# The inversion of 32-blocks in a gated DeltaNet layer: wider scratch transfers, and right operands stored transposed

## The chip, the cores and the metric

The kernel runs on one core of a Trainium2 chip. The metric is the device time of one execution in microseconds; what counts is the median of several runs. All data are fp32; the matrix engine's operands are fp32 too, the large products being split into a high and a low part.

## The reference, cut to what matters

One encoder layer works on a prompt of 1024 tokens and a sample of 256 tokens. A combined projection feeds a bidirectional gated DeltaNet (4 heads, 128 wide) and a differential attention; an output projection, two layer norms and a SwiGLU follow. The change concerns the DeltaNet. Its delta rule is, per head and direction:

```python
decay = jnp.exp(jnp.where(incl, gc[..., :, None] - gc[..., None, :], -jnp.inf))
kb = k * beta[..., None]
m = jnp.where(strict, jnp.einsum('bhnid,bhnjd->bhnij', kb, k) * decay, 0.0)
a_mat = m + jnp.eye(CHUNK, dtype=jnp.float32)
...
sol = lax.linalg.triangular_solve(a_mat, rhs, left_side=True, lower=True, unit_diagonal=True)
...
attn = jnp.einsum('bhnid,bhnjd->bhnij', q, k) * decay
```

A scan over the chunks then carries a 128 x 128 state. So every chunk needs the inverse of a unit triangular matrix.

## The kernel before

**Stages.** Phase A (`phase_a`) projects the input and prepares the DeltaNet: q, k, v, decays, and for every chunk the inverse; the chunk of the kernel has 128 tokens. Phase B runs the scans (`chain`, L974) and the differential attention side by side, phase C the output projection, then the feed-forward part. Phases share on-chip memory: tiles of phase B lie where tiles of phase A lay, and wait for their last reader.

**One preparation.** There are five preparations, one after the other: the four heads of the prompt (8 chunks each) and, as the fifth, the sample, whose 4 heads of 2 chunks are packed as 8 chunks. The texts call them the first to the fifth head. Each has 8 chunks and 2 directions, hence 16 matrices N of 128 x 128, and goes through three generators.

1. The front (`prep_front`, `prep_group`): convolved q, k, v are transposed on TensorE and normalised. Then, for each of two groups of 4 chunks, TensorE forms k·k and k·q in PSUM (L418, tile kq_ps), ScalarE copies them out scaled by -beta (L424) and once unscaled (L426), into the four slots of the tile KQ. The decays are made in place: the cumulated gates are broadcast by DMA into e_f and e_n (L395), masked on VectorE (L406) and exponentiated on ScalarE (L403); e_b is a second masked copy of e_n. VectorE multiplies decays and KQ into N (L435) and into the two attention matrices (L441), which go to the scratch `rec`. The four diagonal 32 x 32 blocks of N go to the scratch `nblk`, one DMA per direction, group and block (L438): 16 a head. kd, the scaled keys, also goes to `rec` (L454).
2. The block inversion (`invert_blocks`): all 64 blocks of 32 x 32 are loaded into the tile Wb with one block per partition, twice (L465), so that 128 partitions work. VectorE builds the inverse U by doubling: 2, 4, 8, 16. Each step is two products by `prod` (L468 to L471): an elementwise multiplication into itmp (L470) and a sum over the last axis (L471); the first product goes into the small tile T, the second into U. The right operand of the first product is a part of U (for 16, copied to R at L495), that of the second is T. Both are held in rows and read by columns: the last axis of the operand has a step of 8 elements (in R and T) or 32 (in U).
3. The levels (`spread_blocks`, `invert_levels`): U goes to the scratch `ublk` (L508), and so does its transpose, which is made in Wb (L509, L510). Both are loaded into the diagonal of the tiles UD, one DMA per orientation, block and direction (L514): 16 a head. Small TensorE products (L535) join 32-blocks to 64 and 64-blocks to 128, with copies between (L545, L559, L565, L572, L573), VectorE scales one result by -beta (L575), and four stores (L578) bring the inverses to `rec`.

**Order.** `advance` moves each of the three lines one step, after each projection block and in its middle; a new block inversion begins when the line is free, and a front goes on to its groups only when fewer than two inversions are under way (`room`). Within this, the order of the instructions on each engine, and of the DMAs on the issue queue of SyncE (SP), is laid out by a planner that follows a simulated timeline (`schedule_with_timeline_sim`), ready instructions with the earliest place in the program first; on the chip each engine and queue keeps that order. The scratch DMAs named above all go through SP. Wb, T, R, U, itmp, UD, KQ and the e tiles have one buffer, N two per direction.

**The end of phase A.** The scans of phase B read `rec` (L969); the first of these loads go into memory that the inversion's tile Z held before.

Of the kernel before, what the change touches and what calls it, by code (L numbers as in the profile page):

```python
# [16 lines left out]
P = 128  # L17
# [317 lines left out]
def prep_front(k, si, vh, c3, G, N, flag, room):  # L335


    nc, V, A, PO = k.nc, k.nc.vector, k.nc.scalar, k.nc.gpsimd
    gp = k.gp1
    raw = gp.tile([P, 2, 8, P], F32, tag="raw", name="raw")  # L340
    ss = gp.tile([P, 2, 8], F32, tag="ss", name="ss")
    for g in range(2):
        u0 = 4 * g
        for role in (0, 1, 2):
            ps = k.pt.tile([P, 512], F32, tag="tp", name="nat_ps")
            for i in range(4):
# [8 lines left out]
        sq = gp.tile([P, 16, P], F32, tag="kq", name="sq")[:, 0:8]  # L355
# [12 lines left out]
    yield  # L368
    while not room():
        yield  # L370
    N.extend(k.gp2.tile([P, 8, P], F32, tag=f"N{d}", name=f"N{d}") for d in range(2))
    for g in range(2):
        yield from prep_group(k, si, vh, g, raw, G, N)


def prep_group(k, si, vh, g, raw, G, N):
    nc, V, A, PO = k.nc, k.nc.vector, k.nc.scalar, k.nc.gpsimd
    rec = k.S.rec[si][vh][g]
    u0 = 4 * g
# [30 lines left out]
    masked(e_f, e_f, k.upper, ALU.add)  # L410
    decay(e_f, 0, 1.0)
    yield
    KQ = gp.tile([P, 4, 4, P], F32, tag="kq", name="KQ")
    for j in range(2):
        ps = k.pg.tile([P, 512], F32, tag="gp", name="kq_ps")
        for i in range(2):
            u = 2 * j + i
            nc.tensor.matmul(ps[:, i * 256:(i + 1) * 256], lhsT=kqT[:, u, 0, :],  # L418
                             rhs=kqT[:, u, :, :].rearrange("p a b -> p (a b)"), start=True, stop=True)
        for i in range(2):  # L420
            u = 2 * j + i
# [12 lines left out]
    def to_blocks(d, e):
        V.tensor_tensor(out=N[d][:, u0:u0 + 4, :], in0=KQ[:, :, 2 * d, :], in1=e, op=ALU.mult)  # L435
        for b in range(4):
            r = slice(32 * b, 32 * b + 32)
            nc.sync.dma_start(out=k.S.nblk[si][vh][d, u0:u0 + 4, b].rearrange("u r c -> r u c"), in_=N[d][r, u0:u0 + 4, r])  # L438

    def attn(d, e):  # L440
        V.tensor_tensor(out=e, in0=KQ[:, :, 1 + 2 * d, :], in1=e, op=ALU.mult)  # L441
        nc.sync.dma_start(out=rec[:, :, 1 + 6 * d, :], in_=e)
# [15 lines left out]
def invert_blocks(k, si, vh):  # L458
# [29 lines left out]
    yield  # L488
    for m in range(2):
        b = m * 528  # L490
        prod(8, 8, 8, (Wb, b + 8, [[32, 8], [0, 8], [1, 8]]), (U, b + 264, [[0, 8], [1, 8], [32, 8]]), (T, 0, [[8, 8], [1, 8]]))
        prod(8, 8, 8, (U, b, [[32, 8], [0, 8], [1, 8]]), (T, 0, [[0, 8], [1, 8], [8, 8]]), (U, b + 8, [[32, 8], [1, 8]]))
    yield
    for hf in range(2):
        V.tensor_copy(view(R, 0, [[8, 16], [1, 8]], 64 * hf, 64), view(U, 528 + 8 * hf, [[32, 16], [1, 8]], 64 * hf, 64))  # L495
    for a in (0, 8):
        prod(8, 8, 16, (Wb, 16 + a * 32, [[32, 8], [0, 8], [1, 16]]), (R, 0, [[0, 8], [1, 8], [8, 16]]), (T, a * 8, [[8, 8], [1, 8]]))
    yield
    for a in (0, 8):
        prod(8, 8, 16, (U, a * 32, [[32, 8], [0, 8], [1, 16]]), (T, 0, [[0, 8], [1, 8], [8, 16]]), (U, 16 + a * 32, [[32, 8], [1, 8]]))  # L500
    return Wb


def spread_blocks(k, si, vh, Wb):

    nc, V, U = k.nc, k.nc.vector, k.Ub
    V.tensor_copy(view(U, 24, [[32, 16], [1, 8]], 0, 64), view(U, 16, [[32, 16], [1, 8]], 64, 64))
    nc.sync.dma_start(out=k.S.ublk[si][vh][0].rearrange("d u b r c -> (d u b) (r c)"), in_=U[0:64])  # L508
    V.tensor_copy(Wb[0:64].rearrange("p (a b) -> p a b", a=32), U[0:64].rearrange("p (b a) -> p a b", a=32))  # L509
    nc.sync.dma_start(out=k.S.ublk[si][vh][1].rearrange("d u b r c -> (d u b) (r c)"), in_=Wb[0:64])  # L510
    for t in (1, 0):
        for b in range(4):
            for d in range(2):
                nc.sync.dma_start(out=diag(k, d, t, b), in_=k.S.ublk[si][vh][t][d, :, b].rearrange("u r c -> r u c"))  # L514


def diag(k, d, t, b):

    c = 32 * b if d == t else 32 * (b % 2)
    return k.UD[d][t][32 * b:32 * b + 32, :, c:c + 32]  # L520


def invert_levels(k, si, vh, N, G):

    nc, V, A, PO = k.nc, k.nc.vector, k.nc.scalar, k.nc.gpsimd
    q = [slice(32 * b, 32 * b + 32) for b in range(4)]
    hq = [slice(32 * (b % 2), 32 * (b % 2) + 32) for b in range(4)]
    uq, dq = (q, hq), (hq, q)
    lo, up = slice(0, 64), slice(64, 128)
    ub = (up, lo)  # L530

    def pe(ps, rows, c0, m, fn):
        for u in range(8):
# [34 lines left out]
    U, D = k.UD[0]  # L568
    r0 = pe(ps, lo, 0, 64, lambda u: (Z[up, 0, u, :], U[up, u, ub[0]]))
    Ub, Db = k.UD[1]  # L570
    r1 = pe(ps, up, 0, 64, lambda u: (Ub[up, u, ub[1]], Z[up, 1, u, :]))
    A.copy(U[lo, :, up], r0)  # L572
    A.copy(Db[up, :, lo], r1)  # L573
    off = 4 * NT[si] + (vh * 8 if si == 1 else 0)
# [17 lines left out]
def phase_a(k):  # L592
    nc, tc = k.nc, k.tc
    with ExitStack() as es:
# [65 lines left out]
        def prep(si, vh, c3):  # L660
# [999 lines left out]
```

## Time and profile before

| | us |
|---|---|
| median of 3 runs | 1794.15 |
| lowest and highest | 1793.14, 1796.1 |
| the profiled execution | 1791.56 |
| its span in the profile | 1789.8 |
| TensorE busy in the span | 1710.3 |
| VectorE busy | 1214.0 |
| ScalarE busy | 783.7 |

In the profile, PE is TensorE's matmul, PEld its weight load, DVE is VectorE, ACT ScalarE, POOL GpSimd and SPq the DMA issue queue of SyncE. A row names line, engine, operation, the written tile, an arrow and the tiles read. Rows of groups end with the count, the busy time in us and the mean of one in ns, and behind a second bar the engine's idle time ahead of them. Rows of a timeline begin with start and duration in us; a bracket gives idle time ahead of the instruction and what ended it.

### The profile page before, as it was taken

The numbers are of one execution on the slowest core, as the hardware profiler recorded it, in microseconds if no ns is written. First come the engines' busy times: TensorE is split into PE (matmuls) and PEld (weight loads), VectorE is DVE, ScalarE is ACT, GpSimd is POOL, SyncE is SP. The second block draws the span as 40 slices with busy tenths as digits, with TensorE's granted clock in tenths as the row PEclk, the third lists the DMA queues.
The fourth block names the chain that finished last, engine by engine and source line by source line (L and its number), as shares of the span: only waits on it lengthen the run. The fifth ranks groups of instructions, "written<-read, shape, count | busy, mean of one in ns | idle before, by whom it ended". The sixth has DMA issues, their size and how long they took to land.

```text
span 1789.8 us, 27447 instructions
## 1 busy us (share of the span) xinstructions
PE 1710.3 (96%) x10234; PEld 1483.0 (83%) x10234; DVE 1214.0 (68%) x2092; ACT 783.7 (44%) x1538; POOL 218.5 (12%) x201
## 2 busy tenths in 40 slices
PE   8999989999986899999999999999999999999998
PEld 8988868888864898788888888888888887888886
DVE  4245888986694468977665866665666665666696
ACT  4146766664433767877113332322222223553330
POOL 2000000000022435732321000000000000000011
PEclk9999999998985999999999999999999999999999
DMA  7124456656754977634631534333344432975541
GB/s 237 40 57 115 126 131 168 168 168 182 190 154 103 297 238 220 177 118 156 188 119 51 193 112 140 120 121 133 124 145 146 146 113 100 386 272 177 174 159 71
DMA packets 254116, 279.05 MB, mean 156 GB/s; under 512 B 49297, under 2 KB 198687, under 8 KB 252575
## 3 DMA queue, kind: packets, MB, share of 16 engines
q1 hardware_dynamic: 244079, 265.20, 47.6%
q10 hardware_dynamic: 9904, 12.10, 2.0%
q8 instruction: 80, 1.31, 0.3%
q14 instruction: 53, 0.43, 0.1%
HBM read 183.80 MB, written 93.43 MB: 155 GB/s over the span
## 4 chain that ended last, share of the span: by engine, by line
PE 54%; ACT 1%; DVE 1%; issue 1%; DMA 0%; POOLq 0%; POOL 0%; DVEq 0%; SPq 0%; ACTq 0%
PE dn_ps L1503 14%; PE gy_ps L1277 9%; PE gs_ps L1277 7%; PE om_ps L172 6%; PE gx_ps L1277 6%; PE gz_ps L1277 6%; PE gp_ps L1277 2%; PE o_ps L875 1%; PE x_ps L1182 0%; ACT ap L839 0%; PE s_ps L835 0%; PE tt_ps L862 0%; PE s_ps L836 0%; DVE ast L837 0%; ACT woh L1162 0%
## 5 line engine op out<-in xcount | busy, mean ns | idle before, releaser
L1293 ACT CAST sph<-wraw 128x512 fp32r<-128x512 f32 x92 | 57.0, 623 | 195.7 <-PE gy_ps L1277 124.5
L310 POOL TENSOR_TENSOR rs_r<-lva,mhalf 128x1 f32<-128x1 f32 x20 | 29.5, 1475 | 837.4 <-DVE lva L1139 818.9
L172 PE MATMUL dps<-xh,wlo 128*128 128x512 f32 (+1 forms) x552 | 122.7, 363 | 2.0 <-DVE wlo L163 2.0
L172 PE MATMUL dps<-xl,whi 128*128 128x512 f32 (+1 forms) x552 | 122.4, 364 | 0.0
L172 PE MATMUL dps<-xh,whi 128*128 128x512 f32 (+1 forms) x552 | 122.2, 362 | 0.0
L1293 ACT CAST sph<-wsum 128x512 fp32r<-128x512 f32 x80 | 49.7, 622 | 156.6 <-PE gy_ps L1277 61.9
L1503 PE MATMUL dn_ps<-tth,ssh 128*128 128x512 f32 x280 | 108.9, 389 | 0.0
L1503 PE MATMUL dn_ps<-ttl,ssh 128*128 128x512 f32 x280 | 108.8, 389 | 0.0
L172 PEld LDWEIGHTS dps<-xh,wlo 128*128 128x128 f32 x552 | 94.4, 193 | 17.3 <-DVE wlo L163 2.4
L1503 PE MATMUL dn_ps<-tth,ssl 128*128 128x512 f32 x280 | 108.1, 389 | 0.0
L172 PEld LDWEIGHTS dps<-xl,whi 128*128 128x128 f32 x552 | 94.8, 195 | 15.8 <-ACT whi L162 0.4
L172 PEld LDWEIGHTS dps<-xh,whi 128*128 128x128 f32 x552 | 94.1, 193 | 14.4
L329 DVE SCALAR_TENSOR_TENSOR c<-pad,cw,c 128x1024 f32<-128x1024 f32 (+1 forms) x96 | 81.7, 876 | 28.8 <-ACT c L327 28.3
L837 DVE TENSOR_REDUCE ast<-s_ps 128x1 f32<-128x1024 f32 (+1 forms) x80 | 83.5, 1055 | 22.6 <-PE s_ps L836 20.4
L1294 DVE TENSOR_TENSOR spl<-wraw,sph 128x512 fp32r<-128x512 f32 x92 | 63.0, 686 | 47.9 <-PE gs_ps L1277 29.6
L839 ACT ACTIVATE ap<-s_ps,ast 128x1024 f32<-128x1024 f32 (+1 forms) x80 | 79.8, 1000 | 34.7 <-DVE ast L837 32.1
L1294 DVE TENSOR_TENSOR spl<-wsum,sph 128x512 fp32r<-128x512 f32 x80 | 55.0, 688 | 46.8 <-issue 20.4
L835 PE MATMUL s_ps<-akl,aq 128*128 128x512 f32 (+1 forms) x144 | 65.8, 458 | 20.3 <-ACT ap L839 19.0
L1494 ACT CAST ssh<-sraw 128x640 fp32r<-128x640 f32 x77 | 55.9, 727 | 48.5 <-PE dn_ps L1503 34.3
L1495 DVE TENSOR_TENSOR ssl<-sraw,ssh 128x640 fp32r<-128x640 f32 x77 | 62.9, 820 | 16.8 <-ACT ssh L1494 13.4
L851 POOL TENSOR_TENSOR ap<-ap,ap 128x512 f32<-128x512 f32 (+2 forms) x60 | 62.4, 1059 | 81.2 <-ACT ap L848 49.5
L875 PE MATMUL o_ps<-av,tt 128*128 128x128 f32 x544 | 66.2, 280 | 0.0
(391 smaller groups left out, 4307.6 us busy)
## 6 DMA issues: line engine op xcount, KB each, us to landing
ld<-rec SPq DMA_DIRECT2D x160, 192.0 KB, 3.9
sraw<-hs SPq DMA_DIRECT2D x77, 320.0 KB, 4.7
wraw<-in_w_gate_up_dram SPq DMA_DIRECT2D x22, 1024.0 KB, 5.2
wraw<-in_w_in_dram SPq DMA_DIRECT2D x24, 512.0 KB, 4.2
wdraw<-in_w_down_dram SPq DMA_DIRECT2D x11, 1024.0 KB, 4.9
ws<-wdraw SPq DMA_DIRECT2D x11, 1024.0 KB, 3.9
traw<-ws SPq DMA_DIRECT2D x44, 256.0 KB, 4.1
araw<-dqk SPq DMA_DIRECT2D x40, 256.0 KB, 5.0
```

The costliest lines, as they stand in the source:

```text
L172: nc.tensor.matmul(out, lhsT=a(i), rhs=b(i), start=start and j == 0, stop=stop and j == len(seq) - 1)
L329: V.scalar_tensor_tensor(out=out, in0=pad[:, so + w:so + w + n], scalar=k.cw[:, w * 12 + ti:w * 12 + ti + 1], in1=out, op0=ALU.mult, op1=A ...
L835: nc.tensor.matmul(ps[:, o:o + w], lhsT=a.q[m][:, qs], rhs=a.kl[m][:, k0 + o:k0 + o + w], start=True, stop=False)
L837: V.tensor_reduce(out=st[:, m:m + 1], in_=ps, op=ALU.max, axis=AX.X, negate=True)
L839: A.activation(p, ps, AF.Exp, bias=st[:, m:m + 1], accum_out=a.s0[:, i:i + 1] if m == 0 else st[:, 2:3])
L851: nc.gpsimd.tensor_tensor(out=pr[0][:, c], in0=pr[0][:, c], in1=pr[1][:, c], op=ALU.add)
L875: nc.tensor.matmul(ps[:, j * P:(j + 1) * P], lhsT=tt[:, i, j * P:(j + 1) * P], rhs=a.v[:, v0 + i, :], start=i == 0, stop=i == NT[a.si] - 1)
L1277: m = nc.tensor.matmul(ps, lhsT=a(i), rhs=b(i), start=start and j == 0, stop=stop and j == len(seq) - 1, skip_group_check=again)
L1293: A.copy(hi, src)
L1294: V.tensor_tensor(out=lo, in0=src, in1=f32(hi), op=ALU.subtract)
L1495: V.tensor_tensor(out=lo, in0=src, in1=f32(hi), op=ALU.subtract)
L1503: nc.tensor.matmul(ps, lhsT=a[:, c], rhs=b, start=z == 0 and j == 0, stop=z == NPR - 1 and j == 2)
```

## The change

- N becomes one tile of 16 matrices, [128, 16, 128], for both directions, with two buffers. The diagonal blocks go to `nblk` once both groups are done, in one DMA per block: 4 a head instead of 16, each with 16 x 32 runs of 128 bytes.
- UD becomes two tiles of [128, 16, 128], one per orientation, with both directions in each. The loads from `ublk` become one per orientation and block: 8 a head instead of 16.
- The transposed copy of U is made in itmp instead of Wb.
- In the block inversion the right operands of the 8- and 16-steps are kept transposed: T is written by columns and read by rows; for the 16-step R is filled transposed; for the 8-step a copy of the part of U into R is new (two a head, 128 x 64 elements). The steps of 2 and 4 stay as they were.
- KQ loses its fourth slot and the unscaled ScalarE copy. VectorE multiplies e_b with k·q straight out of PSUM, in two halves. For that the mask and the exponentials of e_b stand ahead of the KQ products in the program.

The core of the diff:

```diff
-    N.extend(k.gp2.tile([P, 8, P], F32, tag=f"N{d}", name=f"N{d}") for d in range(2))
+    both = k.gp2.tile([P, 16, P], F32, tag="N", name="N")
+    N.extend(both[:, 8 * d:8 * d + 8] for d in range(2))
     for g in range(2):
         yield from prep_group(k, si, vh, g, raw, G, N)
+    for b in range(4):
+        r = slice(32 * b, 32 * b + 32)
+        nc.sync.dma_start(out=k.S.nblk[si][vh][:, :, b].rearrange("d u r c -> r (d u) c"), in_=both[r, :, r])
...
+    e_b = gp.tile([P, 4, P], F32, tag="e_b", name="e_b")
+    masked(e_b, e_n, k.lower, ALU.add)
+    decay(e_b, 1, 1.0)
+    KQ = gp.tile([P, 4, 3, P], F32, tag="kq", name="KQ")
...
-        A.copy(KQ[:, 2 * j:2 * j + 2, 3], ps.rearrange("p (a b c) -> p a b c", a=2, b=2)[:, :, 1])
...
+        V.tensor_tensor(out=e_b[:, 2 * j:2 * j + 2], in0=ps.rearrange("p (a b c) -> p a b c", a=2, b=2)[:, :, 1],
+                        in1=e_b[:, 2 * j:2 * j + 2], op=ALU.mult)
+    nc.sync.dma_start(out=rec[:, :, 7, :], in_=e_b)
...
     def to_blocks(d, e):
         V.tensor_tensor(out=N[d][:, u0:u0 + 4, :], in0=KQ[:, :, 2 * d, :], in1=e, op=ALU.mult)
-        for b in range(4):
-            r = slice(32 * b, 32 * b + 32)
-            nc.sync.dma_start(out=k.S.nblk[si][vh][d, u0:u0 + 4, b].rearrange("u r c -> r u c"), in_=N[d][r, u0:u0 + 4, r])
...
-        prod(8, 8, 8, (Wb, b + 8, [[32, 8], [0, 8], [1, 8]]), (U, b + 264, [[0, 8], [1, 8], [32, 8]]), (T, 0, [[8, 8], [1, 8]]))
-        prod(8, 8, 8, (U, b, [[32, 8], [0, 8], [1, 8]]), (T, 0, [[0, 8], [1, 8], [8, 8]]), (U, b + 8, [[32, 8], [1, 8]]))
+        V.tensor_copy(view(R, 0, [[8, 8], [1, 8]]), view(U, b + 264, [[1, 8], [32, 8]]))
+        prod(8, 8, 8, (Wb, b + 8, [[32, 8], [0, 8], [1, 8]]), (R, 0, [[0, 8], [8, 8], [1, 8]]), (T, 0, [[1, 8], [8, 8]]))
+        prod(8, 8, 8, (U, b, [[32, 8], [0, 8], [1, 8]]), (T, 0, [[0, 8], [8, 8], [1, 8]]), (U, b + 8, [[32, 8], [1, 8]]))
...
-        V.tensor_copy(view(R, 0, [[8, 16], [1, 8]], 64 * hf, 64), view(U, 528 + 8 * hf, [[32, 16], [1, 8]], 64 * hf, 64))
+        V.tensor_copy(view(R, 0, [[16, 8], [1, 16]], 64 * hf, 64), view(U, 528 + 8 * hf, [[1, 8], [32, 16]], 64 * hf, 64))
...
-        prod(8, 8, 16, (Wb, 16 + a * 32, [[32, 8], [0, 8], [1, 16]]), (R, 0, [[0, 8], [1, 8], [8, 16]]), (T, a * 8, [[8, 8], [1, 8]]))
+        prod(8, 8, 16, (Wb, 16 + a * 32, [[32, 8], [0, 8], [1, 16]]), (R, 0, [[0, 8], [16, 8], [1, 16]]), (T, a, [[1, 8], [16, 8]]))
...
-        prod(8, 8, 16, (U, a * 32, [[32, 8], [0, 8], [1, 16]]), (T, 0, [[0, 8], [1, 8], [8, 16]]), (U, 16 + a * 32, [[32, 8], [1, 8]]))
+        prod(8, 8, 16, (U, a * 32, [[32, 8], [0, 8], [1, 16]]), (T, 0, [[0, 8], [16, 8], [1, 16]]), (U, 16 + a * 32, [[32, 8], [1, 8]]))
...
-    V.tensor_copy(Wb[0:64].rearrange("p (a b) -> p a b", a=32), U[0:64].rearrange("p (b a) -> p a b", a=32))
+    V.tensor_copy(k.itmp[0:64].rearrange("p (a b) -> p a b", a=32), U[0:64].rearrange("p (b a) -> p a b", a=32))
...
     for t in (1, 0):
         for b in range(4):
-            for d in range(2):
-                nc.sync.dma_start(out=diag(k, d, t, b), in_=k.S.ublk[si][vh][t][d, :, b].rearrange("u r c -> r u c"))
+            nc.sync.dma_start(out=diag(k, t, b), in_=k.S.ublk[si][vh][t][:, :, b].rearrange("d u r c -> r (d u) c"))
...
-        k.UD = [[per.tile([P, 8, P if d == t else 64], F32, name=f"UD{d}{t}") for t in range(2)] for d in range(2)]
+        k.UD = [per.tile([P, 16, P], F32, name=f"UD{t}") for t in range(2)]
```

The rest of the diff renames the views of UD in the levels, so that every block lies at its place in the full matrix.

More of the change, by code (lines that the diff above doesn't have):

```diff
@@ L435, in to_blocks @@
         V.tensor_tensor(out=N[d][:, u0:u0 + 4, :], in0=KQ[:, :, 2 * d, :], in1=e, op=ALU.mult)
-        for b in range(4):
-            r = slice(32 * b, 32 * b + 32)
[L438 to L442, printed above, removed]
     to_blocks(0, e_f)
-    attn(0, e_f)
+    V.tensor_tensor(out=e_f, in0=KQ[:, :, 1, :], in1=e_f, op=ALU.mult)
+    nc.sync.dma_start(out=rec[:, :, 1, :], in_=e_f)
     yield
-    attn(1, e_b)
     to_blocks(1, e_n)
@@ L508, in spread_blocks, with diag @@
     nc.sync.dma_start(out=k.S.ublk[si][vh][0].rearrange("d u b r c -> (d u b) (r c)"), in_=U[0:64])
-    V.tensor_copy(Wb[0:64].rearrange("p (a b) -> p a b", a=32), U[0:64].rearrange("p (b a) -> p a b", a=32))
-    nc.sync.dma_start(out=k.S.ublk[si][vh][1].rearrange("d u b r c -> (d u b) (r c)"), in_=Wb[0:64])
+    V.tensor_copy(k.itmp[0:64].rearrange("p (a b) -> p a b", a=32), U[0:64].rearrange("p (b a) -> p a b", a=32))
+    nc.sync.dma_start(out=k.S.ublk[si][vh][1].rearrange("d u b r c -> (d u b) (r c)"), in_=k.itmp[0:64])
     for t in (1, 0):
         for b in range(4):
-            for d in range(2):
[L514 to L520, printed above, removed]
+            nc.sync.dma_start(out=diag(k, t, b), in_=k.S.ublk[si][vh][t][:, :, b].rearrange("d u r c -> r (d u) c"))
+def diag(k, t, b, d=None):
+    r = slice(32 * b, 32 * b + 32)
+    return k.UD[t][r, :, r] if d is None else k.UD[t][r, 8 * d:8 * d + 8, r]
 def invert_levels(k, si, vh, N, G):
@@ L526, in invert_levels @@
     q = [slice(32 * b, 32 * b + 32) for b in range(4)]
-    hq = [slice(32 * (b % 2), 32 * (b % 2) + 32) for b in range(4)]
-    uq, dq = (q, hq), (hq, q)
     lo, up = slice(0, 64), slice(64, 128)
-    ub = (up, lo)
+    UD = [[t[:, 8 * d:8 * d + 8] for t in k.UD] for d in range(2)]
     def pe(ps, rows, c0, m, fn):
@@ L549, in invert_levels @@
     for d in range(2):
-        U, D = k.UD[d]
+        U, D = UD[d]
         for x, y in ((0, 1), (2, 3)):
             if d == 0 or x == 2:
-                r = pe(ps, q[x], 256 * d, 32, lambda u: (Z[q[y], d, u, 0:32], diag(k, d, 0, y)[:, u]))
-                out.append((U[q[x], :, uq[d][y]], r))
+                r = pe(ps, q[x], 256 * d, 32, lambda u: (Z[q[y], d, u, 0:32], diag(k, 0, y, d)[:, u]))
+                out.append((U[q[x], :, q[y]], r))
             if d == 1 or x == 0:
-                r = pe(ps, q[y], 256 * d, 32, lambda u: (diag(k, d, 0, y)[:, u], Z[q[y], d, u, 0:32]))
-                out.append((D[q[y], :, dq[d][x]], r))
+                r = pe(ps, q[y], 256 * d, 32, lambda u: (diag(k, 0, y, d)[:, u], Z[q[y], d, u, 0:32]))
+                out.append((D[q[y], :, q[x]], r))
     for i, (o, r) in enumerate(out):
@@ L561, in invert_levels @@
     for d in range(2):
-        U, D = k.UD[d]
+        U, D = UD[d]
         ps = k.pi.tile([P, 512], F32, tag="inv", name="inv_ps")
@@ L567, in invert_levels @@
     ps = k.pi.tile([P, 512], F32, tag="inv", name="inv_ps")
[L568 to L571, printed above, removed]
+    U, D = UD[0]
+    r0 = pe(ps, lo, 0, 64, lambda u: (Z[up, 0, u, :], U[up, u, up]))
+    Ub, Db = UD[1]
+    r1 = pe(ps, up, 0, 64, lambda u: (Ub[up, u, up], Z[up, 1, u, :]))
     A.copy(U[lo, :, up], r0)
@@ L619, in phase_a @@
             nc.gpsimd.memset(pad, 0.0)
-        k.UD = [[per.tile([P, 8, P if d == t else 64], F32, name=f"UD{d}{t}") for t in range(2)] for d in range(2)]
-        for row in k.UD:
-            for t in row:
-                nc.gpsimd.memset(t, 0.0)
+        k.UD = [per.tile([P, 16, P], F32, name=f"UD{t}") for t in range(2)]
+        for t in k.UD:
+            nc.gpsimd.memset(t, 0.0)
         k.upper, k.lower = [per.tile([P, P], F32, name=n) for n in ("m_up", "m_low")]
@@ L668, in invert @@
             def invert():
-                flag.Wb = yield from invert_blocks(k, si, vh)
+                yield from invert_blocks(k, si, vh)
             def back():
-                spread_blocks(k, si, vh, flag.Wb)
+                spread_blocks(k, si, vh)
                 yield from invert_levels(k, si, vh, N, k.G[si])
```

12 lines of the change are left out of this document (3 added, 9 removed).

## The prediction

> **What bounds the kernel now.** First the page, for the engines' shares and for the second part, the span in 40 slices of 44.7 us.
>
> ```profile
> span 1789.8 us, 27447 instructions
> PE 1710.3 (96%) x10234; PEld 1483.0 (83%) x10234; DVE 1214.0 (68%) x2092; ACT 783.7 (44%) x1538; POOL 218.5 (12%) x201
> PE   8999989999986899999999999999999999999998
> PEclk9999999998985999999999999999999999999999
> ```
>
> TensorE is busy almost everywhere except in slices 11 and 12 (about 490 to 580 us), where its clock also falls to half. That is where the input projection ends and attention begins. The change touches only instructions ahead of 580 us, so I look at that stretch by windows, cut at its landmarks (columns: length, busy time and count per engine, granted clock, DMA share, GB/s).
>
> ```profile
> 225.00:345.00 120.00, 111.78 (x759) 95.78 (x760) 109.44 (x162) 79.30 (x176) 9.55 (x5) 0.96 0.59 156
> 345.00:420.00 75.00, 70.59 (x575) 60.68 (x573) 55.58 (x91) 41.06 (x94) 2.95 (x2) 0.91 0.61 160
> 420.00:492.00 72.00, 70.65 (x611) 60.53 (x611) 50.32 (x87) 36.68 (x86) 0.00 (x0) 0.98 0.71 196
> 492.00:523.00 31.00, 28.66 (x191) 25.52 (x190) 28.28 (x56) 9.71 (x15) 4.85 (x2) 0.89 0.58 159
> 523.00:584.00 61.00, 36.27 (x273) 26.97 (x272) 34.80 (x40) 23.93 (x35) 16.30 (x11) 0.55 0.48 121
> 584.00:855.00 271.00, 252.58 (x1889) 234.46 (x1889) 195.70 (x409) 198.74 (x435) 118.25 (x129) 0.98 0.66 202
> ```
>
> The reader should see three things. Until 523 TensorE is full (111.78 of 120, 70.65 of 72). From 523 to 584 it does 36 us of work in 61 us at 0.55 of its clock: that is the hole. After 584 it is full again (252.58 of 271, 93%), so whatever starts this part earlier moves the end nearly as much. What holds the hole open is read from the timelines of the fourth and fifth inversions (the DMA issue queue SP, then VectorE, then TensorE).
>
> ```profile
> 467.76 2.16 SPq L438 DMA_DIRECT2D nblk<-N  x4
> 475.80 10.22 SPq L514 DMA_DIRECT2D UD<-ublk  x16
> 486.07 1.14 SPq L465 DMA_DIRECT2D Wb<-nblk  x2
> 492.17 0.18 DVE L474 COPY Ub<-Wb 128x16 f32<-128x16 f32 x1 [7.86 <-issue]
> 539.77 0.56 SPq L508 DMA_DIRECT2D ublk<-Ub  x1
> 544.85 8.94 SPq L514 DMA_DIRECT2D UD<-ublk  x16
> 547.60 1.93 PE L535 MATMUL inv_ps<-UD,N 32*32 32x32 f32 x32 [1.10 <-DMA UD<-ublk]
> 573.04 1.59 PE L535 MATMUL inv_ps<-Z,UD 64*64 64x64 f32 x13
> 574.66 0.83 SPq L969 DMA_DIRECT2D ld<-rec  x2
> 583.57 0.77 PE L1023 MATMUL vn_ps<-ld,ld 128*128 128x128 f32 x2 [8.94 <-DMA ld<-rec]
> ```
>
> This is one chain. The fifth head's blocks are in scratch soon after 469.9, but their load stands behind sixteen UD loads of the fourth head and goes at 486.07. VectorE, idle for 7.86 us, then inverts from 492.17 to 539.77, when the result is stored; sixteen UD loads follow; the level matmuls run from 547.60 to 574.6; the scan's first loads go at 574.66, at the last level matmul, and its first matmul runs at 583.57. **The end of the fifth inversion is the bound of this stretch**, and so the change is worth what it takes from that chain.
>
> **Part 1, the products on VectorE.** The products of the 8- and 16-blocks read their right operand with a step of 8 to 32 elements; after the change it is stored transposed and read in runs.
>
> ```profile
> L470 DVE TENSOR_TENSOR itmp<-Ub,iT 128x1024 f32<-128x1024 f32 x10 | 22.4, 2243 | 0.1
> L470 DVE TENSOR_TENSOR itmp<-Wb,iR 128x1024 f32<-128x1024 f32 x10 | 21.1, 2113 | 0.3
> L470 DVE TENSOR_TENSOR itmp<-Ub,iT 128x512 f32<-128x512 f32 x10 | 11.3, 1126 | 0.2
> L470 DVE TENSOR_TENSOR itmp<-Wb,Ub 128x512 f32<-128x512 f32 x10 | 10.9, 1089 | 0.3
> L575 DVE TENSOR_TENSOR UD<-UD,nbeta 128x1024 f32<-128x1024 f32 x5 | 6.1, 1218 | 2.3 <-ACT UD L573 2.3
> L441 DVE TENSOR_TENSOR e_b<-KQ,e_b 128x512 f32<-128x512 f32 x10 | 6.8, 684 | 0.0
> L509 DVE COPY Wb<-Ub 64x1024 f32<-64x1024 f32 x5 | 5.5, 1098 | 0.1
> L507 DVE COPY Ub<-Ub 64x128 f32<-64x128 f32 x5 | 1.1, 222 | 0.2
> L761 DVE TENSOR_TENSOR rx<-rx,rcs 128x256 f32<-128x256 f32 x5 | 2.1, 419 | 3.6 <-DMA rx<-dqk 3.6
> ```
>
> Each form runs twice per head. With runs I price them like the contiguous products of their size, 1218 and 684 ns: 2 x (2243 + 2113 + 1126 + 1089) = 13.14 us becomes 8 products for 4 x 1.218 + 4 x 0.684 = 7.61, a saving of 5.53 us per head. Added: two copies of 128x64 into R, 0.22 each by the 222 ns row, 0.44; the two old R copies become transposing, which the transposing L509 copy prices at 1098/1024 = 1.07 ns an element, so about 0.1 more. The e_b product is split in two, 4 x 0.419 instead of 2 x 0.684 per head, 0.31 more. (No row of this shape reads PSUM; between half of 684 and all of it, the split costs from 0 to 1.4.) Net 4.7 us per head, 23 for five; between a loss of 0.85, if the step was not the cause, and 5.5.
>
> The reduces now write T with a step; no row shows that. Its bounds are nothing (L509 reads with a step of 32 elements at the one-element rate) and one extra 1.04 ns cycle for each of 8 x 64 written elements, 0.5 us a head; I take nothing. [...]
>
> How much of it lies on the chain? The last two inversions run with the projection's convolutions done, and VectorE is the engine they wait for (28.28 of 31 us busy from 492 to 523): 2 x 4.7 = 9.4 in full. The first three share a VectorE that is full (109.44 of 120) with a TensorE that is as full; I count half, 7.0. Together 16.4.
>
> **Part 2, the loads and stores on the SP queue.** Per head 16 nblk stores become 4 and 16 UD loads become 8, with the same number of 128-byte runs. What was issued around the fourth head, and what such transfers take (the first two rows give the issue time as min/median/max in ns, the others KB and median us to landing):
>
> ```profile
> L514 SPq DMA_DIRECT2D UD<-ublk x80: 303/449/1673, 261.5 to 553.3; - x80
> L578 SPq DMA_DIRECT2D rec<-UD x20: 512/634/802, 309.8 to 578.5; - x20
> UD<-ublk SPq DMA_DIRECT2D x80, 32.0 KB, 1.9
> nblk<-N SPq DMA_DIRECT2D x80, 16.0 KB, 2.3
> rec<-UD SPq DMA_DIRECT2D x20, 256.0 KB, 3.4
> 417.32 1.14 SPq L465 DMA_DIRECT2D Wb<-nblk  x2
> 421.99 0.18 DVE L474 COPY Ub<-Wb 128x16 f32<-128x16 f32 x1 [4.49 <-issue]
> ```
>
> A wide UD load has 512 runs, as many as a rec<-UD store (128 partitions x 4), which issues in 634 ns against 449; with the gaps between I take 0.7 us each, 5.6 for eight, where the rows show 10.22 and 8.94 for sixteen. So the next head's block load, which stands behind them, goes about 4.6 us earlier. VectorE sat idle 7.86 and 4.49 us for exactly that load before heads five and four, so 4.6 + 4.5 = 9.1 counts; before heads two and three it had other work, and I count nothing. In the fifth head the levels' first two groups need the first and third load rather than the first six: 6 x 0.56 less 3 x 0.7, about 1.3, and the last load lands 3.3 us earlier; 2.0 for both. Sum 11.1, between 0 (if a load twice as wide also takes twice as long to issue; the 634 ns row is against it) and 20 (rival 1). The loads' own landing should stay between the 1.9 us of now and the 3.4 us of a rec<-UD store, eight times as many bytes.
>
> Against it: the nblk stores now leave only when both groups are done, behind the second group's kd stores. That adds one longer store at the end, 4 x 0.7 against 2.16, and up to 1.1 us of landing, 1.7 us. For the fifth head the 16 us between 469.9 and 486.07 cover it; if that cover goes, it costs 1.7. I charge 2.
>
> **Part 3, what is moved in the preparation.** ScalarE loses the third KQ copy; e_b's mask and exponentials go ahead of the KQ matmul, and VectorE multiplies straight out of PSUM. The row to price it:
>
> ```profile
> L403 ACT ACTIVATE e_b<-e_b,ngc 128x128 f32<-128x128 f32 x40 | 12.8, 391 | 5.5 <-DVE e_b L406 5.5
> ```
>
> The copy leaves an engine that is not full (36.68 of 72 us from 420 to 492), worth nothing in itself. The exponentials (4 x 0.391) now stand ahead of the KQ evacuation on ScalarE, and behind them wait that evacuation and the copies that empty the projection's PSUM banks. I take nothing for it (ScalarE waited only 5.5 us over all of them); its upper price is rival 3. A gain is excluded as long as VectorE and SP carry the chain. The two UD tiles are larger and cleared on GpSimd before the first inversion; that engine is busy 12% of the span, so nothing.
>
> **Sum.** 16.4 + 11.1 - 2 = 25.5 us earlier for the scan's start. Not all of it is gained: TensorE used the hole for 36.27 us of work at 0.55 clock, 20 us at full clock, and 25.5/61 of that, 8.3, must now be done later. Net **17 us**. The profiled execution took 1791.56 us (1.8 beyond its span), 2.6 below the median of 1794.15; 1774.5 on its scale is **1777 us** as a median.
>
> **Rivals.** (1) *The block load overtakes the UD loads.* The transposed copy now lies in itmp, so Wb is free once the products end, and the fifth load could go near 473 rather than 486: 9 us beyond my 4.6. The levels would then run beside the projection, at full clock, where their first group takes less:
>
> ```profile
> 479.77 1.17 PE L535 MATMUL inv_ps<-UD,N 32*32 32x32 f32 x32 [0.61 <-DMA UD<-ublk]
> ```
>
> 1.17 us against 1.93 makes some 10 of 27 us. With the last part given back (about 2), 1777 - 9 - 10 + 2 = 1760. Against it: the order on SP is set by a planner, which so far put the block load last. Chance 0.17.
>
> (2) *TensorE paces it.* It is 94% busy from 225 to 523; if the fronts wait for their transposes in its stream, VectorE's savings turn into idle time, and only the fifth head's last steps count, about 5 us: 1789, anywhere from 1784 to 1796. Chance 0.15. Close by: *the products do not get faster*, because the zero-step left operand and not the right one costs the second cycle. No L470 row has a right operand in runs, so this is open. Then 11.1 - 2 is left, less the added 0.85 a head in the share of part 1 (3.0), less a third given back: 4, and 1790. Chance 0.07.
>
> (3) *Slower: ScalarE waits for e_b.* If the e_b mask comes late on a full VectorE, ScalarE stands in front of the KQ and projection evacuations, and TensorE runs out of PSUM banks. The price of a stop is read at the worst one of now:
>
> ```profile
> 265.00:270.00 5.00, 1.31 (x25) 1.31 (x26) 3.00 (x3) 2.43 (x3) 5.00 (x1) 0.57 0.50 93
> 270.00:275.00 5.00, 4.58 (x49) 3.99 (x47) 4.14 (x7) 1.06 (x1) 0.87 (x2) 0.50 0.70 143
> ```
>
> 3.69 us idle there, and 0.43 x 5 + 0.50 x 5 = 4.7 us of clock lost with it: each microsecond costs two. Stops of 1.3 us in ten groups would cost 26, 9 more than the forecast gains: 1803. It decides from about 0.85 us a group. [...] Against the rival also speaks that e_f's exponentials already stand there. Chance 0.13.
>
> **Numbers.** The forecast has 0.48 (its own range 1768 to 1785). This kernel's measurement tells about 0.2%, 3.6 us, from no change. Faster: 0.48 + 0.17, 0.06 of rival 2 and 0.04 of its neighbour, 0.75. Within: the rest of these two, 0.12. Slower: 0.13. The range of 8 in 10 reaches from a little under rival 1, 1757, to the slow end of rival 2, 1796.
>
> **What would show it.** L470 at 128x1024 near 1.22 us and at 128x512 near 0.69 (part 1); eight UD loads in under 6 us and the fifth L474 before 480 (part 2); the first scan matmul near 558 instead of 583.57, the hole from the projection's end to it shorter and less at half clock. I am wrong if L470 stays above 2 us, if the fifth L474 stays after 488, if TensorE gains new stops on KQ or projection banks, or if the scan starts 25 us earlier and the part behind it grows by as much.

## The result and the profile after

The changed kernel takes 1761.34 us (median of four runs, 1760.14 to 1765.65) against 1793.64 of the kernel before (four, 1792.85 to 1796.1): a ratio of 0.9825, with a 95% interval of 0.9806 to 0.9843. It is faster by 32 us, where 17 was forecast; the time lies within the range, and 1.3 us from the time that rival 1 gave. The profiled execution took 1765.65 us, the slowest of its four; against the 1791.56 of before it gains 26. The 6 us between the two differences lie between executions, and no view explains them.

On the page of the changed kernel, the same lines as before:

```profile
span 1763.8 us, 27355 instructions
PE 1705.1 (97%) x10234; PEld 1479.4 (84%) x10234; DVE 1193.9 (68%) x2112; ACT 779.9 (44%) x1520; POOL 221.0 (13%) x199
PE   8999999999998999999999999999999999999998
PEclk9999998999996999999999999999999999999999
```

Of the trough in the TensorE line (8, 6 and 8 tenths in slices 12 to 14, counted from one; the prediction counts from nought) one slice at 8 is left, and in the trough the clock falls in slice 13 only, to 6 tenths, where slices 12 and 13 had 8 and 5. VectorE has lost 20 us of work. Cut at the new landmarks, the windows show the stretch that the prediction spoke of (columns as there):

```profile
225.00:345.00 120.00, 115.61 (x829) 99.47 (x829) 103.46 (x174) 84.60 (x177) 10.54 (x5) 0.96 0.62 166
345.00:420.00 75.00, 73.50 (x651) 63.54 (x650) 53.75 (x108) 42.30 (x102) 2.89 (x1) 0.98 0.60 171
420.00:492.00 72.00, 67.49 (x489) 56.46 (x488) 55.93 (x122) 27.38 (x65) 0.00 (x0) 0.93 0.63 181
...
515.00:558.00 43.00, 33.31 (x288) 26.93 (x287) 23.44 (x29) 22.73 (x34) 14.58 (x10) 0.60 0.59 144
558.00:829.00 271.00, 254.44 (x1895) 234.85 (x1895) 199.93 (x414) 200.53 (x438) 119.51 (x129) 0.98 0.69 206
```

Two things have moved. The hole, from the projection's last matmul to the scan's first, is 39 us wide instead of 61 (517 to 556 against 523 to 584; the row above takes in 2 us on either side). And from 225 to 420 TensorE is fuller (189 of 195 us busy against 182); the projection's last matmul ends at 517 instead of 523. The last window, 271 us from a little behind the scan's start, is what it was: 254 us busy then, 253 before.

The chain of the fourth and fifth head, from the same timelines as in the prediction (start, length, instruction; SP, VectorE and TensorE by time; products are now L469, the block load L464, the UD loads L512, the scan's first matmul L1017):

```profile
455.13 2.23 SPq L377 DMA_DIRECT2D nblk<-N  x4
460.12 0.48 SPq L464 DMA_DIRECT2D Wb<-nblk  x1
461.49 0.74 SPq L464 DMA_DIRECT2D Wb<-nblk  x1
464.81 4.18 SPq L512 DMA_DIRECT2D UD<-ublk  x8
467.62 0.17 DVE L473 COPY Ub<-Wb 128x16 f32<-128x16 f32 x1
508.69 0.91 SPq L507 DMA_DIRECT2D ublk<-Ub  x1
509.64 0.59 SPq L509 DMA_DIRECT2D ublk<-itmp  x1
510.91 2.24 SPq L573 DMA_DIRECT2D rec<-UD  x2
514.31 1.51 SPq L573 DMA_DIRECT2D rec<-UD  x2
516.94 5.23 SPq L512 DMA_DIRECT2D UD<-ublk  x8
549.40 2.72 SPq L963 DMA_DIRECT2D ld<-rec  x6
555.94 0.76 PE L1017 MATMUL vn_ps<-ld,ld 128*128 128x128 f32 x2 [4.60 <-DMA ld<-rec]
```

The fifth head's block load goes at 460.12, ahead of the fourth head's UD loads; before, it went at 486.07, behind sixteen. Its inversion starts 24.6 us earlier (467.62 against 492.17), takes 41.1 us up to its store instead of 47.6, and the scan starts 27.6 us earlier (555.94 against 583.57). The wide transfers can be measured here too: eight UD loads take 4.18 and 5.23 us, where the prediction's rows have 10.22 and 8.94 for sixteen.

VectorE's groups between 60 and 640 us (busy us, mean ns of one, idle before):

```profile
L469 DVE TENSOR_TENSOR itmp<-Ub,iT 128x1024 f32<-128x1024 f32 x10 | 13.0, 1302 | 0.1
L469 DVE TENSOR_TENSOR itmp<-Wb,iR 128x1024 f32<-128x1024 f32 x10 | 12.2, 1222 | 0.2
L469 DVE TENSOR_TENSOR itmp<-Wb,iR 128x512 f32<-128x512 f32 x10 | 6.9, 692 | 0.3
L469 DVE TENSOR_TENSOR itmp<-Ub,iT 128x512 f32<-128x512 f32 x10 | 6.8, 682 | 0.0
L470 DVE TENSOR_REDUCE iT<-itmp 128x64 f32<-128x1024 f32 x10 | 12.2, 1218 | 0.2
L490 DVE COPY iR<-Ub 128x64 f32<-128x64 f32 x10 | 2.1, 213 | 0.2
L433 DVE TENSOR_TENSOR e_b<-kq_ps,e_b 128x256 f32<-128x256 f32 x20 | 8.2, 420 | 9.0 <-ACT KQ L431 9.0
```

The four product groups fell from 65.7 to 38.9 us. The new copies into R take 0.21 us each, and the product out of PSUM 420 ns, as the 419 ns row of another product had priced it.

### The profile page after: what moved, and what is told of

Read it like the earlier page. It is cut to its first block, busy times and chain, and to the rows that moved or that the text cites. A ratio compares the mean times of both kernels' runs of the same rounds, so it can differ in the third digit from the quotient of the medians.

```text
span 1763.8 us, 27355 instructions
## 1 busy us (share of the span) xinstructions
PE 1705.1 (97%) x10234; PEld 1479.4 (84%) x10234; DVE 1193.9 (68%) x2112; ACT 779.9 (44%) x1520; POOL 221.0 (13%) x199
## 4 chain that ended last, share of the span: by engine, by line
PE 55%; DVE 1%; issue 1%; DMA 1%; ACT 0%; POOLq 0%; POOL 0%; DVEq 0%; SPq 0%
PE dn_ps L1497 15%; PE gy_ps L1271 9%; PE gs_ps L1271 7%; PE gx_ps L1271 6%; PE om_ps L172 6%; PE gz_ps L1271 6%; PE gp_ps L1271 2%; PE o_ps L869 1%; PE x_ps L1176 0%; DMA worw<-in_w_out_dram 0%; PE tt_ps L856 0%; PE s_ps L829 0%; ACT ap L833 0%; PE s_ps L830 0%; DVE ast L831 0%
## 5 line engine op out<-in xcount | busy, mean ns | idle before, releaser
L172 PE MATMUL dps<-xh,whi 128*128 128x512 f32 (+1 forms) x552 | 126.1, 363 | 0.0
L172 PEld LDWEIGHTS dps<-xh,whi 128*128 128x128 f32 x552 | 95.0, 192 | 14.7
L831 DVE TENSOR_REDUCE ast<-s_ps 128x1 f32<-128x1024 f32 (+1 forms) x80 | 83.6, 1057 | 31.8 <-PE s_ps L830 29.8
L845 POOL TENSOR_TENSOR ap<-ap,ap 128x512 f32<-128x512 f32 (+2 forms) x60 | 63.3, 1075 | 51.5 <-ACT ap L842 24.6
```

Of the source, the lines that this page charges most:

```text
L172: nc.tensor.matmul(out, lhsT=a(i), rhs=b(i), start=start and j == 0, stop=stop and j == len(seq) - 1)
L831: V.tensor_reduce(out=st[:, m:m + 1], in_=ps, op=ALU.max, axis=AX.X, negate=True)
L845: nc.gpsimd.tensor_tensor(out=pr[0][:, c], in0=pr[0][:, c], in1=pr[1][:, c], op=ALU.add)
```

## The experiments

**What was to be told apart.** Theory A is the prediction's: the parts add up along the chain that ends at the scan's start. Its rivals said that one part carries most of the gain (the block load let past the UD loads), that the slack beside the chain swallows most of what is saved on it, or that it counts only in the last head. The texts on record name them by letters of their own. Each run is given as a ratio to the kernel before on the same chip, with its interval, and compared with the change's 0.9825 where it starts from the changed kernel; a thousandth is 1.8 us. The figure that most runs turn on is the start of the scan's first matmul, since span less start is 1206.2 us before and 1207.9 after, and between 1204 and 1209 in all other profiles but two: **the scan's start sets the end, nearly one to one.** The two are runs 3 and 8, with 1212.4 and 1211.4: there the scan starts 4.2 and 7.4 us earlier than before (579.4 and 576.2), and the part behind it is 6.2 and 5.2 us longer, so that most or all of it is given back.

**1. The products alone**, in the kernel before:

```diff
+        V.tensor_copy(view(R, 0, [[8, 8], [1, 8]]), view(U, b + 264, [[1, 8], [32, 8]]))
-        prod(8, 8, 8, (Wb, ...), (U, b + 264, [[0, 8], [1, 8], [32, 8]]), (T, 0, [[8, 8], [1, 8]]))
+        prod(8, 8, 8, (Wb, ...), (R, 0, [[0, 8], [8, 8], [1, 8]]), (T, 0, [[1, 8], [8, 8]]))
...
```

> The kernel before with the transposed right operands alone (part 1); transfers, itmp and preparation as before. Theory A (the inversion chain is the bound, and each part shortens it by its own share): L470 at 128x1024 falls from 2.1 to about 1.22 us, VectorE does about 24 us less before the scans, and the scan's first matmul comes 12 to 17 us earlier than 583.6: about 1778 to 1782 against 1794. Rival B (the block load that overtakes the UD loads makes the gain, since Wb is free earlier): the fifth L474 stays behind sixteen UD loads and the gain is under 6 us. Rival C (any shorter chain lets the planner lay out the whole stretch anew, and shares mean nothing): anything from no gain to the whole 30 us.

Measured: 0.9924 (0.9904 to 0.9943), 14 us faster; the scan starts at 566.93, 16.6 us earlier. SP and VectorE around the fourth head:

```profile
465.54 9.09 SPq L515 DMA_DIRECT2D UD<-ublk  x16
474.67 1.12 SPq L465 DMA_DIRECT2D Wb<-nblk  x2
480.53 0.18 DVE L474 COPY Ub<-Wb 128x16 f32<-128x16 f32 x1 [5.81 <-issue]
```

The block load is still last, and VectorE still waits 5.81 us for it. So this is the share of part 1 with the queue as it was, and its 16.6 us meet the 16.4 that the prediction counted: 11.6 come before the fifth inversion starts (11.7 were counted), 3.0 in it up to its store (4.7 were counted), and 2.0 behind it, where none were.

**2. The products undone in the changed kernel** (the same edit backwards).

> The changed kernel with the right operands of the 8 and 16 steps read with a step again, as before (part 1 undone). Theory A: loses 12 to 17 us of the 32, about 1773 to 1778. Rival B: loses less than 6 us. Rival C: anything between no loss and all.

Measured: 0.9855 (0.9831 to 0.988); the four groups take 2280, 2116, 1137 and 1082 ns again, the scan starts at 560.72. The fifth head's block load goes behind the fourth's UD loads here (466.46, they end at 462.15). The loss is 0.0030 with some 0.0031 either way (the half-widths of both intervals, added in quadrature): 5 us, between none and 11. The expectation fails: what gives 14 alone is missed by 5. The parts are not terms of one sum.

**3. The transposed copy in itmp alone**, in the kernel before, and **4. the same copy put back into Wb** in the changed kernel:

```diff
-    V.tensor_copy(Wb[0:64].rearrange("p (a b) -> p a b", a=32), U[0:64].rearrange("p (b a) -> p a b", a=32))
+    V.tensor_copy(k.itmp[0:64].rearrange("p (a b) -> p a b", a=32), U[0:64].rearrange("p (b a) -> p a b", a=32))
```

> The kernel before with only the transposed copy of U moved from Wb to itmp. Theory A: the next block load may go up to ten us sooner, but VectorE's work and sixteen UD loads remain: 2 to 5 us gained. Rival B: 8 to 15 us gained, fifth block load ahead of the fourth head's UD loads. Rival C: anything between.

> The changed kernel with the transposed copy of U made in Wb again, so that the next block load must wait for the store of it. Theory A: loses 2 to 6 us. Rival B: loses 10 us or more, the block loads go behind the UD loads again. Rival C: anything.

Alone it is worth nothing that can be told (0.9992, 0.9981 to 1.0004), so rival B's 8 to 15 us are excluded: the loads overtook before two earlier heads, but the fifth's still went behind the fourth's UD loads, at 484.48. What it stood behind there were the fifth head's own last nblk stores, issued from 480.19 to 483.21 after those UD loads. Taken from the changed kernel it costs 0.0048, with 0.0025 either way, 9 us (ratio 0.9873, 0.9856 to 0.9889), between the two expectations. SP and VectorE there:

```profile
459.50 2.09 SPq L513 DMA_DIRECT2D UD<-ublk  x4
462.61 2.26 SPq L513 DMA_DIRECT2D UD<-ublk  x4
468.03 1.87 SPq L464 DMA_DIRECT2D Wb<-nblk  x2
473.37 0.18 DVE L473 COPY Ub<-Wb 128x16 f32<-128x16 f32 x1 [11.71 <-issue]
```

The load is behind the eight UD loads again, and VectorE idles 11.71 us in front of the fifth inversion, which starts 5.8 us later than in the changed kernel. So the overtaking is worth something only once the rest has made room for it.

**5. Sixteen UD loads again** and **6. sixteen nblk stores again**, each in the changed kernel, and **7. the wide nblk stores alone** in the kernel before:

```diff
-            nc.sync.dma_start(out=diag(k, t, b), in_=k.S.ublk[si][vh][t][:, :, b].rearrange("d u r c -> r (d u) c"))
+            for d in range(2):
+                nc.sync.dma_start(out=diag(k, t, b, d), in_=k.S.ublk[si][vh][t][d, :, b].rearrange("u r c -> r u c"))
```

```diff
-    for b in range(4):
-        r = slice(32 * b, 32 * b + 32)
-        nc.sync.dma_start(out=k.S.nblk[si][vh][:, :, b].rearrange("d u r c -> r (d u) c"), in_=both[r, :, r])
...
+        for b in range(4):
+            r = slice(32 * b, 32 * b + 32)
+            nc.sync.dma_start(out=k.S.nblk[si][vh][d, u0:u0 + 4, b].rearrange("u r c -> r u c"), in_=N[d][r, u0:u0 + 4, r])
```

> The changed kernel with the UD loads cut per direction again: sixteen a head, 8 on each side of the merge. Theory D (chain, with the loads as one of its links): about 4 us of issue come back before the fifth block load or, where that load goes first, behind it, and 2 to 4 us in the fifth head: loses 5 to 10 us, about 1767 to 1771. Rival E (the transfers' number is hidden; it is the preparation, part 3, that made the rest of the gain): loses under 2 us.

> The changed kernel with the nblk stores per direction and group again, sixteen a head, issued as each product is ready. Theory D: SP gets 12 more issues of half a microsecond a head, of which only the last few lie ahead of a block load: loses 0 to 4 us. Rival E: no change within 2 us. Rival F (leaving late costs, the wide stores wait for both groups): gains 1 to 4 us.

> The kernel before with the N tile for both directions and the four wide nblk stores a head alone; UD loads, Wb, products and preparation as before. The prediction charged these stores with 2 us. Theory H (the sixteen narrow stores were themselves in the way, between other issues on SP and ahead of the block loads): 5 to 12 us faster than before. Rival I (wide stores help only when Wb is free early, so that the block load is waiting for them): within 3 us of before.

Run 5 gives 0.9852 (0.982 to 0.9885), 5 us with almost 7 either way: inconclusive. In its profile the sixteen loads stand behind the block load, where they delay nobody's inversion, and the scan starts at 551.79, 4.2 us earlier than in the changed kernel's profile. So no run shows a gain of the merged UD loads in the changed kernel. Run 6 gives 0.9874 (0.9849 to 0.9899), 9 us lost, with 6 either way, where 0 to 4 was expected. SP and VectorE of run 6:

```profile
459.31 4.72 SPq L512 DMA_DIRECT2D UD<-ublk  x6
...
465.24 2.04 SPq L441 DMA_DIRECT2D nblk<-N  x4
468.75 1.80 SPq L464 DMA_DIRECT2D Wb<-nblk  x2
474.15 0.18 DVE L473 COPY Ub<-Wb 128x16 f32<-128x16 f32 x1 [5.39 <-DMA Wb<-nblk]
```

The last narrow stores of the fifth head now stand behind the UD loads of the fourth, and the block load behind both: 474.15 against 467.62. In this profile most of it is made up, and the scan starts at 557.47, only 1.5 us later: the fourth head's stores are issued before 510 here, and from the store of U to the scan's first load it takes 34.0 us instead of 40.7. Run 7 gives 0.9971 (0.9956 to 0.9987), 5 us gained by the wide stores alone. Both ratios agree in sign: fewer stores were a gain, not the loss that was charged. Merging the UD loads alone in the kernel before wasn't tried.

**8. Part 3 alone** (e_b ahead of the KQ matmul, three KQ slots) in the kernel before:

```diff
-        A.copy(KQ[:, 2 * j:2 * j + 2, 3], ps.rearrange("p (a b c) -> p a b c", a=2, b=2)[:, :, 1])
+        V.tensor_tensor(out=e_b[:, 2 * j:2 * j + 2], in0=ps.rearrange("p (a b c) -> p a b c", a=2, b=2)[:, :, 1],
+                        in1=e_b[:, 2 * j:2 * j + 2], op=ALU.mult)
```

> The kernel before with part 3 alone: e_b prepared ahead of the KQ products and multiplied out of PSUM by VectorE, the unscaled ScalarE copy gone, KQ with three slots. Theory D: within 3 us of before, since ScalarE is not in the chain. Rival E: 10 to 20 us faster than before.

Measured: 0.9985 (0.9971 to 0.9999), 3 us faster. Rival 3 is refuted where the other parts don't cover it.

**9 and 10. Time added to the chain**: the changed kernel with its transposed copy made ten times instead of once, in the fifth head only (`si == 0`), then in the first head only (`si == 1 and vh == 0`).

```diff
+    for _ in range(10 if si == 0 else 1):
-    V.tensor_copy(k.itmp[0:64].rearrange("p (a b) -> p a b", a=32), U[0:64].rearrange("p (b a) -> p a b", a=32))
+        V.tensor_copy(k.itmp[0:64].rearrange("p (a b) -> p a b", a=32), U[0:64].rearrange("p (b a) -> p a b", a=32))
```

> The changed kernel with the transposed copy of U (1.1 us) done ten times instead of once, in the fifth head alone: nine copies, 9.9 us of VectorE, ahead of the store of the transpose; the result is the same. Theory A (the end of the fifth inversion is the bound, one to one): 9 to 10 us slower than the changed kernel. Rival G (TensorE's work sets the start of the scans, or the hole gives half of it back, as the prediction's last term assumed): 3 to 7 us slower.

> The changed kernel with the transposed copy of U done ten times in the first head alone, about 10 us of VectorE ahead of that head's UD loads. Theory A in the form of the prediction (a microsecond in the first three inversions counts half): 4 to 6 us slower than the changed kernel. Rival J (early inversions are hidden by the later fronts and by TensorE's projection): under 2 us slower. Rival K (VectorE is one long queue, every microsecond counts): 9 to 12 us slower.

In the fifth head: 0.9913 (0.9884 to 0.9942), 16 us lost with 6 either way. On its VectorE (the last seven copies), SP and TensorE:

```profile
518.01 7.42 DVE L509 COPY itmp<-Ub 64x1024 f32<-64x1024 f32 x7
525.46 0.49 SPq L510 DMA_DIRECT2D ublk<-itmp  x1
528.83 1.90 SPq L513 DMA_DIRECT2D UD<-ublk  x4
566.82 0.77 PE L1018 MATMUL vn_ps<-ld,ld 128*128 128x128 f32 x2 [10.80 <-issue]
```

The transposed blocks are stored 15.8 us later (525.46 against 509.64). Of these, 3.1 lie ahead of the added copies (U itself is stored at 511.83 against 508.69), in the order that the planner laid anew. About 5 are absorbed on the spot, for in the changed kernel the UD loads waited for the fourth head's stores until 516.94 anyway; the scan starts 10.9 us later. So the chain is the bound, and what is late on it is late at the end; the size is 10 to 22 us by the ratios and 7 by the two profiled executions. In the first head: 0.9889 (0.9869 to 0.991), 11 us lost with 5 either way; the next head's inversion starts 20 us later:

```profile
280.47 1.12 DVE L509 COPY itmp<-Ub 64x1024 f32<-64x1024 f32 x1
282.69 0.18 DVE L473 COPY Ub<-Wb 128x16 f32<-128x16 f32 x1
```

(282.69 against 262.38; the row above is the last of the ten copies, between which VectorE did other work.) Much of the 20 us is made up by the fifth head, and the scan starts at 562.17, 6.2 us later than in the changed kernel's profile. Nine copies last 10 us: by the ratios 6 to 16 of them arrive at the end, by the two profiled executions 6, so more than half, and perhaps all.

**11 and 12. The chain put first.** If the chain sets the end, its instructions should go ahead of others. In the changed kernel the block inversions, and in run 12 the levels too, get a raised priority in the planner:

```diff
-            stage_of(blocks_, levels)
+            stage_of(blocks_, levels, HP_F)
```

> The changed kernel with the block inversions emitted at the same raised priority as the fronts, so that the planner puts block loads and products ahead of the other work on SP and VectorE. Theory A: the block load of the fourth and fifth head goes sooner after its nblk stores and VectorE spends less time on other work within an inversion: 3 to 10 us faster than the changed kernel. Rival G (the fronts bound the chain now, raising the inversions delays them): no gain or some us slower.

> As the one before, with the levels at the raised priority too: their matmuls and copies go ahead of the attention scores in the hole. Theory A: a further 2 to 6 us, since the last levels took 40 us from the store of U to the scans' first load. Rival L (the levels wait for their own loads and for TensorE at half clock, not for a place in the queues): no further gain.

Run 11 takes 1752.78 us, 0.9768 (0.9743 to 0.9794): 10 us faster than the changed kernel, with 6 either way, and the fastest version here. Its chain on SP, VectorE and TensorE:

```profile
446.81 1.14 SPq L464 DMA_DIRECT2D Wb<-nblk  x2
453.18 4.61 SPq L512 DMA_DIRECT2D UD<-ublk  x8
453.24 0.18 DVE L473 COPY Ub<-Wb 128x16 f32<-128x16 f32 x1 [1.31 <-DMA ublk<-Ub]
497.52 0.48 SPq L507 DMA_DIRECT2D ublk<-Ub  x1
...
533.12 2.72 SPq L963 DMA_DIRECT2D ld<-rec  x6
539.27 0.77 PE L1017 MATMUL vn_ps<-ld,ld 128*128 128x128 f32 x2 [3.52 <-DMA ld<-rec]
```

The fifth inversion starts 14.4 us earlier (453.24), and the scan 16.7. Run 12 gives 0.9795 (0.9768 to 0.9821): raising the levels too adds nothing, and whether it loses is not told by these intervals.

## Why the prediction was right, and where it was not

The direction and the mechanism stand: the end of the fifth inversion is the bound, the change shortens what leads to it, and the scan's start carries it to the end (runs 9 and 11 move it in both directions). The forecast is 16 us short by the medians, and 9 by the profiled executions. The 9 by its own steps, in us:

| step | forecast | profiled |
|---|---|---|
| fifth inversion starts earlier (7.0 + 4.7 + 9.1 - 2) | 18.8 | 24.6 |
| the inversion itself, to its store, is shorter | 4.7 | 6.5 |
| from its store to the scan's first load | 2.0 shorter | 5.8 longer |
| from there to the scan's first matmul | 0 | 2.4 shorter |
| scan starts earlier | 25.5 | 27.6 |
| given back behind it | 8.3 | 1.6 |
| span | 17 | 26.0 |

**Part 1.** The prices were right: 1222 and 682 to 692 ns against 1218 and 684 forecast; the 1302 of one group has its cause in the last section. So was its count of 16.4 in the kernel before (16.6 in run 1). "I count half" for the first heads looks too little in the changed kernel (run 10: 6 to 16 of 10). Yet there the parts overlap: without the products it loses only 5 us (run 2). How the rest of the 14 is made up there isn't settled; the planner lays the whole order anew with each edit.

**The stepped reduces.** "I take nothing" held: the reduce that writes T with a step takes 1218 ns, and took 1215 when it wrote in rows. (The bound of 8 x 64 elements counted all eight reduces of a head; only four write T, so it was half as large. Its 1.04 ns is what an element costs between the products of 684 and 1218 ns, 534 ns for 512 more.) The products' right operand is where the step showed: 2113 ns with it and 1222 without.

**Part 2.** The step "4.6 earlier" failed in the good direction for the fifth head: the load did not go behind shorter UD loads but ahead of them. That is rival 1's order, given 0.17; the planner that "so far put the block load last" took the other order once Wb was free early enough. Wb alone was not enough: with the products (run 2), the copy (run 4) or the wide stores (run 6) undone, the load falls behind the UD loads again, and the fifth inversion starts at 473.92, 473.37 and 474.15, some 6 us later each time. The overtaking needs all three, which fits parts that do not add up. Before the fourth head it still went behind eight of them (issued from 397.58 to 402.45, the load at 405.10), and VectorE's wait fell from 4.49 to 1.08 us, much as priced. So the fourth inversion starts 9.9 us earlier (412.13 against 421.99) and the fifth 24.6; most of the surplus arose between the two (14.7 us, where 4.7 + 4.6 were counted). "Before heads two and three it had other work" does not hold for the third: VectorE waited 2.59 us for its load. The eight loads themselves took 4.2 to 5.2 us where 5.6 was taken. The charge of 2 for the nblk stores had the wrong sign: alone the wide stores gain 5 (run 7). The prediction priced their later departure and not the twelve issues that leave the queue.

**The fifth head's end** was to become 2.0 shorter and became 5.8 longer. The fourth head's stores, four rec<-UD at 510.91 to 515.82, stand on SP ahead of the fifth head's UD loads, so these go 8.2 us behind the store instead of 5.1; and the levels take 32.5 instead of 29.8 us. In rival 1 this was where another 10 us were to come from, at full clock. They did not come; that its 1760 was met is partly chance, since the missing 10 were made up elsewhere.

**"8.3 must now be done later"** is the step that cost the forecast most. It took the matmuls done in the hole for work that would have to follow later. What fills the hole of that kind are attention's score products; these two rows count their pairs from 500 us to the scan's start, the first before, the second after:

```profile
L835 PE MATMUL s_ps<-akl,aq 128*128 128x512 f32 x22 | 14.3, 651 | 10.7 <-ACT ap L839 9.4 <-POOL akl L163 1.3
```

```profile
L829 PE MATMUL s_ps<-akl,aq 128*128 128x512 f32 x18 | 10.8, 601 | 2.7 <-ACT ap L833 2.7
```

22 pairs against 18: the idle time in the first row is for ap, ScalarE's result, which fits work that had run as far ahead as its buffers let it, in the hole of before. The other profiles agree: ten of the fourteen have just 22 pairs ahead of the scan, whether it starts at 549.68 (run 12) or at 583.57, and before, the last pair went 21 us ahead of it:

```profile
562.36 0.63 PE L835 MATMUL s_ps<-akl,aq 128*128 128x512 f32 x1
```

By the prediction's own measure the narrower hole still held 29.31 us of matmuls at 0.59 of the clock, 17 us at full clock, 3 less than the 20 of before and not 8. Only four pairs are pushed back, and the part behind the scan's start is 1.6 us longer, where 8.3 was counted. That part does not follow the number of pairs, though: run 5 has 12 pairs ahead of its scan and 1208.3 us behind the start, runs 3 and 8 have 22 and 1212.4 and 1211.4. Why work pushed back costs so little stays open.

**The other rivals.** TensorE does not pace it (0.15): from 225 to 420 it became busier, not later. The products did get faster (0.07). ScalarE made nobody slower (0.13; run 8).

## What to carry to other kernels

Find the event whose shift moves the end one to one (here: span less start, the same in almost every profile), add time to its chain at two places to see what counts there, and then give that chain's instructions priority: the last step was one argument and 10 us. On SP the number of issues was a cost for whoever stood behind: sixteen UD loads took 10.22 us ahead of the fifth head's block load, eight took 4.87 ahead of the fourth's after the change. A merged transfer was worth what it let go ahead, so one edit alone may show nothing (the copy in itmp, 0.9992) and still be needed (0.0048 lost without it). Before charging work in a hole as "done later", see whether its buffers had already stopped it.

## What the runs showed of the hardware

**The clock in the hole.** Windows of 5 us in the changed kernel (last three columns: granted clock, DMA share, GB/s):

```profile
525.00:530.00 5.00, 5.00 (x69) 4.09 (x67) 4.36 (x7) 0.68 (x1) 0.00 (x0) 0.50 0.97 192
530.00:535.00 5.00, 5.00 (x66) 4.45 (x64) 1.40 (x3) 4.64 (x8) 4.56 (x3) 0.50 0.14 37
```

TensorE counts as busy for ten microseconds on end (the profile models the matmuls' ends, so short gaps can be hidden), and its clock stays at half, 0.50 in both windows. The work here is that of the levels, in tiles of 32, between attention's matmuls; whether the small tiles are the cause was not tried.

**VectorE beside GpSimd.** Two answers of the changed kernel's timeline, GpSimd first:

```profile
501.76 2.52 POOL L163 TENSOR_TENSOR akl<-araw,akh 128x1024 fp32r<-128x1024 f32 x1 [96.85 <-ACT akh L162]
510.31 2.40 POOL L163 TENSOR_TENSOR akl<-araw,akh 128x1024 fp32r<-128x1024 f32 x1 [6.03 <-ACT akh L162]
```

```profile
500.80 1.23 DVE L469 TENSOR_TENSOR itmp<-Ub,iT 128x1024 f32<-128x1024 f32 x1
502.06 1.22 DVE L470 TENSOR_REDUCE Ub<-itmp 128x64 f32<-128x1024 f32 x1
503.32 2.04 DVE L469 TENSOR_TENSOR itmp<-Ub,iT 128x1024 f32<-128x1024 f32 x1
...
511.52 2.27 DVE L570 TENSOR_TENSOR UD<-UD,nbeta 128x1024 f32<-128x1024 f32 x1 [2.19 <-ACT UD L568]
```

While GpSimd works on the first, to 504.28, VectorE's reduce takes its usual 1.22 us, but the product that starts at 503.32 takes 2.04: 0.82 more, nearly the 0.96 us for which the two overlap. With x10 in the group, this one adds 82 ns to its mean, which is the 1302 against 1222. It ends 1.08 us behind the GpSimd instruction. The other product that starts within a GpSimd instruction here, at 511.52, takes 2.27 us where the other four of its line take 1.22, and ends 1.08 behind it too, while the product that had started before the first one, at 500.80, keeps its 1.23. So these two seem to have done nearly all their work only when GpSimd was done. It does not always go so: in the kernel before, a product of the second form starts at 521.99, within a GpSimd instruction that lasts from 521.10 to 525.45, and takes 1.23 us. No run was made to test it.
